# The second half of an output projection as Strassen's seven block products

## The chip, the cores and the metric

The kernel runs on one core of one Trainium2 chip. The metric is the device time of one execution in microseconds (us). Before the change it is 972.64 us, the median of 3 runs (972.55 to 972.85).

## The reference

A trunk of two decoder layers works on one sequence of 512 tokens with 1024 channels, in float32. The part that matters here is layer 1's mixer and what follows it:

```python
proj = gelu(einsum('bsd,de->bse', rms_norm(h, norm_mix[1]), w_in_odd[0]))
u, v = proj[..., :1024], proj[..., 1024:]
mix = chunked_spatial_gating(u, v, sgu_norm[0], w_spatial[0], b_spatial[0])
h = h + einsum('bse,ed->bsd', mix, w_out_odd[0])        # the output projection
hn = rms_norm(h, norm_ffn[1])
h = h + gated_conv_ffn(hn, w_ffn_gate[1], w_ffn_up[1], conv_ffn[1], b_conv_ffn[1], w_ffn_down[1])
return rms_norm(h, final_norm)
```

Layer 0 has another mixer of the same size, an output projection of the same kind, and an FFN of the same form. The hidden width of the FFN is 2816.

## The kernel before

The residual `h` is held as 8 tiles `h0` to `h7` of 128 channels by 512 tokens, float32. Every matrix product is done in float32 by three matmuls: each operand is split into a high part (rounded to the matmul's float32r) and a low part (what rounding left out), and `mm3` (lines 156 to 159) adds high by high, high by low and low by high. For weights, `parts` makes the high part by a copy on ScalarE and the low part by a subtraction on VectorE. `summed` makes the low part without VectorE: ScalarE writes the negated high part and a DMA on GpSimd's queue adds the float32 weights onto it.

Weights come through rotating buffers in the pool `wp`: 4 float32 buffers `raw`, 6 `whi` and 6 `wlo`, each of 128 partitions by 1024 elements. SyncE issues the fetches. A fetch waits until a raw buffer is free, and a split waits until a `whi` and a `wlo` buffer are free. TensorE writes to 7 PSUM banks (`mm_bank`) and one for small things.

The order of instructions on each engine is fixed when the kernel is built, by a planner that goes by the order of the program text and by its own estimate of when each operand will be ready; `inorder` and `behind` pin a few of them.

Layer 1's mixer (`mixer1`) ends like this. The group `u1` computes the last 512 columns of the input projection. Between its matmuls stand the spatial products (`spatial`) and the first transposes: `turned(j)` turns tile j of the gated product from tokens by channels to channels by tokens through TensorE (line 1106), and splits it into the high and low parts `mx` (lines 1108 and 1109). Tiles 0 to 3 are turned during `u1`, tiles 4 to 7 during the first blocks of the output projection by the hook `second_half`. The output projection is `project("oo", ...)`, in two halves of 4 output tiles. Each half takes 4 weight chunks of 256 by 512 elements and runs 4 outputs x 8 blocks x 3 = 96 matmuls of 512 tokens. The last 4 blocks are done output by output (`tail=4`), so that the outputs become ready one after another. When output tile k is ready, VectorE adds it to `h` (line 315) and `Norm.add` writes the split `hg[k]` of `h` times the gain (ScalarE line 202, VectorE line 203), squares `h` on ScalarE (lines 209 and 212), and adds the square to `ssq` on GpSimd (line 213). `hg[0]` to `hg[7]` are the FFN's moving operands.

The FFN of layer 1 (`ffn1`, `Ffn`) follows. Its first step (`direct`) multiplies with plain matmuls over the pairs 0, 4, 1, 5, 2, 6, 3, 7 and turns the residual back (`turn_residual`, line 1187) in between. From its second step on (f = 2) the FFN already works by Strassen's seven products, in the helper `multiply`: tokens are cut into two blocks of 256, and the sums over `hg` and over the weights are prepared by `block_sums` and `prepare`. One product of step f = 2 is 12 matmuls of 256 tokens (line 581). The table `BANK` says which products share a PSUM bank: 1, 6, 7 and 4 accumulate in one, 5 and 3 in another, 2 has its own.

Of the kernel before, what the change touches and what calls it, by code (L numbers as in the profile page):

```python
# [8 lines left out]
F32 = mybir.dt.float32  # L9
F32R = mybir.dt.float32r  # L10
BF16 = mybir.dt.bfloat16
AF = mybir.ActivationFunctionType
ALU = mybir.AluOpType
PSUM = bass.MemoryType.PSUM

P = 128
D = 1024
S = 512
NK = D // P
# [12 lines left out]
def tile_trunk(ctx: ExitStack, tc: tile.TileContext, x, norm_mix, norm_ffn, final_norm,  # L32
# [3 lines left out]
    nc = tc.nc  # L36
    x = x[0]
# [92 lines left out]
    def fetch(src, a, b, name):  # L130
        raw = wp.tile([P, a, b], F32, tag="raw", bufs=4, name=f"raw_{name}")
        nc.sync.dma_start(raw, src)
        return raw, a, b, name
# [52 lines left out]
    h = [cp.tile([P, S], F32, tag=f"h{k}", name=f"h{k}") for k in range(NK)]  # L186
    hg2 = [cp.tile([P, 2, S], F32R, name=f"hg{k}") for k in range(NK)]
    hg = [(t[:, 0], t[:, 1]) for t in hg2]
# [114 lines left out]
    def project(name, w, acts, ks, norm, before=None, halves=(0, 1), tail=4):  # L303

        for gi in halves:
            chunks = half_weights(name, w, ks, gi)

            def lhs(k, j):
                hi, lo, n = chunks[k]
                cs = slice(j * P, (j + 1) * P)  # L310
                return hi[:, n, cs], lo[:, n, cs]

            def done(j, ps):
                k = gi * 4 + j
                nc.vector.tensor_tensor(h[k], ps, h[k], ALU.add)  # L315
                if norm is not None:
                    norm.add(k)

            group(f"{name}{gi}", range(4), ks, lhs, lambda k, j: acts[k], tail, done,
                  before if gi == 0 else None)  # L320
# [221 lines left out]

    STEPS = [(0, None, True), (2, (0, 2, 0), False), (4, (0, 2, 1), True)]
    for f in range(6, NF, 4):
        STEPS += [(f, (f - 4, f, 0), False), (f + 2, (f - 4, f, 1), f + 4 < NF)]
    HALF = S // 2
    NP = NK // 2
# [42 lines left out]
    class Ffn:  # L592
# [109 lines left out]
        def moving(self, product, kp):  # L702

            if product in (1, 2, 3):
                k = kp if product == 1 else kp + NP
                c = slice(HALF, S) if product == 3 else slice(0, HALF)
                return hg[k][0][:, c], hg[k][1][:, c]
            if product in (6, 7):
                t = self.t23[kp][product - 6]
                return t[:, 0, :], t[:, 1, :]  # L710
            return tuple(t[:, {4: 0, 5: 1}[product], :] for t in self.t41[kp])
# [186 lines left out]
    def mixer1(norm):  # L898
        w = w_in_odd[0]
        with tc.tile_pool(name="m1", bufs=1) as mp:  # L900
# [27 lines left out]
            banks = v_group(0, {(4, 0): lambda: norm.rstd_cols(inorder)})  # L928
# [46 lines left out]
            class InProducts:  # L975
# [19 lines left out]
                def put(self, product, how, at):  # L995
                    self.stat[product] = [how(raw, 2, 512, f"{self.name}_{product}_{n}")
                                          for n, raw in enumerate(self.raw[at])]
# [18 lines left out]
                def multiply(self, banks, i, product):  # L1016
                    at = BANK[product], i
                    first = at not in banks
                    if first:
                        banks[at] = mm_bank(f"{self.name}_{at[0]}{i}")  # L1020
                    left = tokens(product, i)
                    for kp in range(NP):
                        lhs = left(kp)
                        rhs = [x[:, kp % 2, :] for x in self.stat[product][kp // 2]]
                        for l, r, end in ((0, 0, False), (0, 1, False), (1, 0, kp == NP - 1)):
                            nc.tensor.matmul(banks[at], lhs[l], rhs[r], start=first, stop=end,  # L1026
                                             skip_group_check=True)
                            first = False
                    return banks[at]
# [29 lines left out]
            v = [mp.tile([P, D], F32, tag="v", bufs=4, name=f"v{t}") for t in range(NT)]  # L1059
# [13 lines left out]
                                                   op0=ALU.mult, op1=ALU.subtract)  # L1073
                vn.append((hi, lo))

            u, gt, mix = {}, {}, {}

            def by_chunk(ap):
                return ap.rearrange("p (n c) -> p n c", c=P)
# [19 lines left out]
            def turned(j):  # L1099
                half, i = j // 4, j % 4  # L1100
                if i == 0:
                    mix["t", half] = [mp.tile([P, 4, S], F32R, tag="vn", bufs=4,
                                              name=f"mx{half}_{n}") for n in range(2)]
                ps = mm_bank(f"mT{j}")
                for t in range(NT):
                    nc.tensor.transpose(ps[:, t * P : (t + 1) * P], gt[j][:, t, :], ident)
                hi, lo = (x[:, i, :] for x in mix["t", half])
                nc.scalar.activation(hi, ps, AF.Copy)
                nc.vector.tensor_tensor(lo, ps, hi.bitcast(F32), ALU.subtract)
                mix[j] = hi, lo  # L1110

            u[0] = mp.tile([P, NT, S], F32, tag="u", bufs=2, name="u0")

# [49 lines left out]
            def second_half(k):  # L1163
                if 1 <= k < 4:
                    for j in ((4,), (5,), (6, 7))[k - 1]:
                        turned(j)

            nxt = Norm("f1", lambda k: prm1("ffn", k))
            project("oo", w_out_odd[0], mix, list(range(NK)), nxt, before=second_half)
            return nxt  # L1170


# [274 lines left out]
```

## Time and profile before

| | |
|---|---|
| median of 3 runs | 972.64 us |
| profiled execution | 972.66 us |
| its span, first to last instruction | 970.9 us |
| mean granted TensorE clock | 0.998 |
| TensorE busy | 961.0 us (99%) |
| VectorE busy | 812.9 us (84%) |
| ScalarE busy | 597.5 us (62%) |
| GpSimd busy | 152.0 us (16%) |

In the profile PE is TensorE's matmuls, PEld its weight loads, DVE VectorE, ACT ScalarE, POOL GpSimd, and SPq and POOLq the DMA issues on SyncE's and GpSimd's queues. Times are microseconds from the start of the span. A row of the timeline gives start, duration, engine, line of the kernel, and the operation with its output, inputs and shape; a bracket tells how long the engine had been idle and what released it. A row of a window gives the length of the stretch and each engine's busy time in it with its count of instructions, then the granted clock, the DMA engines' busy share and GB/s. Matmuls are pipelined, so the distance between two starts tells more than the duration of one.

### The profile page before, as it was taken

To read this page: it belongs to the slowest core of one execution; us is meant where nothing else is said; L and a number is where in the kernel's file an instruction comes from. 1 tells how busy PE (TensorE), PEld (TensorE's weight loads), DVE (VectorE), ACT (ScalarE), POOL (GpSimd) and SP (SyncE) were. 2 spreads that over 40 slices of the span, in tenths; PEclk is the share of its full clock that TensorE was granted. 3 is DMA by queue.
4 is the path that set the end of the run, shared out by engine and by line. 5 is a ranking of instruction groups with operands and counts; after the bars stand their busy time and mean duration, and the time that the engine had idled before them with its cause. 6 is when DMAs were issued, how large, how long until landed. Compare 5 with 4: busy or idle time off the path is not lost.

```text
span 970.9 us, 13658 instructions
## 1 busy us (share of the span) xinstructions
PE 961.0 (99%) x4952; PEld 818.6 (84%) x4952; DVE 812.9 (84%) x1387; ACT 597.5 (62%) x895; POOL 152.0 (16%) x173
## 2 busy tenths in 40 slices
PE   9999999999999999999999999999999999999996
PEld 7888888988888888888888888889888888888885
DVE  6887458999898998998878675589998989889897
ACT  5523347765675665765586834587665666656775
POOL 3141023110111010110311001221111011100123
PEclk9999999999999999999999999999999999999999
DMA  7442225776777677774352333167767777668775
GB/s 252 149 137 86 87 88 111 178 180 161 195 175 168 157 174 195 168 176 135 128 153 87 109 109 108 51 136 182 185 142 196 195 174 174 159 162 200 195 154 139
DMA packets 92335, 148.33 MB, mean 153 GB/s; under 512 B 5124, under 2 KB 56300, under 8 KB 92268
## 3 DMA queue, kind: packets, MB, share of 16 engines
q1 hardware_dynamic: 76236, 98.69, 32.1%
q0 software_dynamic: 14256, 46.93, 26.8%
q10 hardware_dynamic: 1776, 1.84, 0.6%
q8 instruction: 39, 0.64, 0.3%
q14 instruction: 28, 0.23, 0.1%
HBM read 98.42 MB, written 2.10 MB: 104 GB/s over the span
## 4 chain that ended last, share of the span: by engine, by line
PE 94%; DVE 3%; DMA 1%; issue 1%; ACT 0%; POOLq 0%; DVEq 0%; POOL 0%
PE dn L158 3%; PE dn L159 3%; PE dn L157 3%; PE d L158 3%; PE d L157 3%; PE d L159 3%; PE vu_a L1026 2%; PE gu L157 2%; PE gu L159 2%; PE oo L159 2%; PE oo L157 2%; PE gu L158 2%; PE oe L159 1%; PE oe L158 1%; PE oo L158 1%; PE oe L157 1%
## 5 line engine op out<-in xcount | busy, mean ns | idle before, releaser
L144 POOL DMA_DIRECT2D wlo_g<-raw_g x20 | 17.2, 862 | 318.8 <-ACT wlo_g L142 118.3
L617 DVE SCALAR_TENSOR_TENSOR c<-rows,prm,c 128x512 f32<-128x512 f32 x88 | 65.3, 744 | 1.6 <-ACT c L615 1.4
L158 PE MATMUL dn<-wlo_dn,a_hi 128*128 128x512 f32 x144 | 56.2, 390 | 0.0
L158 PE MATMUL d<-a_lo,whi_d 128*128 128x512 f32 x144 | 56.2, 390 | 0.0
L159 PE MATMUL dn<-whi_dn,a_lo 128*128 128x512 f32 x144 | 56.2, 390 | 0.0
L159 PE MATMUL d<-a_hi,wlo_d 128*128 128x512 f32 x144 | 56.1, 390 | 0.0
L157 PE MATMUL d<-a_hi,whi_d 128*128 128x512 f32 x144 | 56.1, 390 | 0.0
L157 PE MATMUL dn<-whi_dn,a_hi 128*128 128x512 f32 x144 | 56.1, 390 | 0.0
L731 ACT ACTIVATE whi_a<-raw_g 128x512 fp32r<-128x512 f32 x20 | 12.6, 632 | 61.3 <-PE g_10e L571 9.0
L213 POOL TENSOR_TENSOR ssq_f<-ssq_f,sq_f 128x512 f32<-128x512 f32 x14 | 19.8, 1411 | 142.4 <-issue 102.0
L142 ACT ACTIVATE wlo_g<-raw_g 128x1024 fp32r<-128x1024 f32 x20 | 21.2, 1062 | 27.5 <-PE g_2e L581 8.8
L202 ACT ACTIVATE hg<-h,prm 128x512 fp32r<-128x512 f32 x24 | 17.3, 721 | 33.1 <-DVE h L315 33.1
L615 ACT ACTIVATE c<-rows,prm 128x512 f32<-128x512 f32 x44 | 31.4, 715 | 9.8 <-DVE rows L828 9.6
L625 ACT ACTIVATE s<-c,prm 128x512 f32<-128x512 f32 x44 | 31.4, 716 | 6.2 <-DVE c L617 6.1
L1201 DVE SCALAR_TENSOR_TENSOR y<-dn,small,y 128x512 f32<-128x512 f32 x40 | 28.0, 749 | 8.1 <-PE dn L159 8.1
L203 DVE SCALAR_TENSOR_TENSOR hg<-h,prm,hg 128x512 fp32r<-128x512 f32 x24 | 22.6, 944 | 11.9 <-ACT hg L202 11.9
L159 PEld LDWEIGHTS dn<-whi_dn,a_lo 128*128 128x128 f32 x144 | 27.0, 188 | 5.7
L159 PEld LDWEIGHTS d<-a_hi,wlo_d 128*128 128x128 f32 x144 | 27.0, 188 | 5.7
L153 DVE TENSOR_TENSOR wlo_dn<-raw_dn,whi_dn 128x1024 fp32r<-128x1024 f32 x18 | 22.0, 1224 | 11.7 <-ACT whi_dn L152 10.6
L157 PEld LDWEIGHTS d<-a_hi,whi_d 128*128 128x128 f32 x144 | 27.1, 188 | 5.4
L157 PEld LDWEIGHTS dn<-whi_dn,a_hi 128*128 128x128 f32 x144 | 27.1, 188 | 5.4
L158 PEld LDWEIGHTS dn<-wlo_dn,a_hi 128*128 128x128 f32 x144 | 27.0, 188 | 5.4
(1060 smaller groups left out, 3261.6 us busy)
## 6 DMA issues: line engine op xcount, KB each, us to landing
raw_g<-in_w_ffn_gate_dram SPq DMA_DIRECT2D x40, 512.0 KB, 3.8
raw_u<-in_w_ffn_up_dram SPq DMA_DIRECT2D x40, 512.0 KB, 4.3
raw_dn<-in_w_ffn_down_dram SPq DMA_DIRECT2D x22, 512.0 KB, 6.0
wlo_g<-raw_g POOLq DMA_DIRECT2D x20, 512.0 KB, 4.6
wlo_u<-raw_u POOLq DMA_DIRECT2D x20, 512.0 KB, 6.4
raw_d<-in_w_ffn_down_dram SPq DMA_DIRECT2D x18, 512.0 KB, 4.1
wlo_s12g<-s12g POOLq DMA_DIRECT2D x18, 512.0 KB, 6.3
wlo_s34g<-s34g POOLq DMA_DIRECT2D x18, 512.0 KB, 5.7
```

Of the source, the lines that this page charges most:

```text
L142: first = nc.scalar.activation(lo, raw, AF.Copy, scale=-1.0)
L153: behind(nc.vector.tensor_tensor(lo, raw, hi.bitcast(F32), ALU.subtract), after[0])
L157: nc.tensor.matmul(ps, lhs[0], rhs[0], start=start, stop=False)
L158: nc.tensor.matmul(ps, lhs[0], rhs[1], start=False, stop=False)
L159: nc.tensor.matmul(ps, lhs[1], rhs[0], start=False, stop=stop)
L203: nc.vector.scalar_tensor_tensor(hg[k][1], h[k], g, hg[k][0].bitcast(F32), op0=ALU.mult, op1=ALU.subtract)
L213: nc.gpsimd.tensor_tensor(self.ssq, self.ssq, sq, ALU.add)
L615: nc.scalar.activation(c, t[:, 0:S], AF.Copy, scale=prm("cf", ft))
L617: self.last_conv = nc.vector.scalar_tensor_tensor(c, t[:, i : S + i], prm("cf", i * NF + ft), c, op0=ALU.mult, op1=ALU.add)
L625: self.last_silu = nc.scalar.activation(s, c, AF.Silu, bias=self.prm("bf", ft))
L1026: nc.tensor.matmul(banks[at], lhs[l], rhs[r], start=first, stop=end, skip_group_check=True)
L1201: return nc.vector.scalar_tensor_tensor(dst, ps, ffn.cols[:, t : t + 1], dst, op0=ALU.mult, op1=ALU.add)
```

## The change

The first half of layer 1's output projection stays. The second half (output tiles 4 to 7) is cut into blocks: output channels in two of 256, input channels in two of 512, tokens in two of 256. It is computed by seven block products in the order 1, 2, 6, 5, 7, 3, 4, each for two output tiles of 128 channels, and each of these is 12 matmuls of 256 tokens.

- The weights are fetched as 4 blocks of 512 by 256. `parts` splits the weights of products 1, 2, 4 and 6, `summed` those of 5, 7 and 3. Four sums of blocks are made in place on VectorE.
- `turned` also writes a float32 copy of each turned tile (`mr`, in the buffers of the tag `v`) on ScalarE.
- `sums_of`, called from the hook at blocks 4 and 5 of the first half, makes the sums of token blocks in place on VectorE. Two of the four sums are split into `hg[4]` to `hg[7]`, which are free at that time (products 6 and 5); the other two into new tiles `t43` in the buffers of the tag `u` (products 4 and 7), with the low part by ScalarE and a DMA on GpSimd's queue.
- After each product VectorE adds the bank to half a tile of `h`, 14 additions of 256 tokens. After products 3 and 4 `norm.add` follows for the tile.

```diff
+    def block_sums_of(y0, y1):
+        t3, t1, t2, t4 = y1[:, :, HALF:], y0[:, :, HALF:], y0[:, :, :HALF], y1[:, :, :HALF]
+        nc.vector.tensor_tensor(t3, t3, t1, ALU.subtract)
+        nc.vector.tensor_tensor(t1, t1, t2, ALU.subtract)
+        nc.vector.tensor_tensor(t2, t2, t3, ALU.add)
+        nc.vector.tensor_tensor(t4, t4, t2, ALU.subtract)
+
+    def project_blocks(name, w, acts, sums, norm):
+        raw = {}
+        for i, j in ((0, 0), (1, 0), (1, 1), (0, 1)):
+            raw[i, j] = fetch(w[i * 512 : (i + 1) * 512, 512 + j * HALF : 512 + (j + 1) * HALF]
+                              .rearrange("(k p) c -> p k c", p=P), 4, HALF, f"{name}_{i}{j}")
+        stat = {}
+        def put(product, how, at):
+            r, a, b, n = raw[at]
+            stat[product] = how(r, a, b, f"{n}_{product}")
+        def to(at, x, y, op):
+            nc.vector.tensor_tensor(raw[at][0], raw[x][0], raw[y][0], op)
+
+        a11, a12, a21, a22 = (0, 0), (1, 0), (0, 1), (1, 1)
+        put(1, parts, a11)
+        put(2, parts, a12)
+        put(4, parts, a22)
+        to(a22, a21, a22, ALU.add)
+        to(a21, a11, a21, ALU.subtract)
+        to(a11, a22, a11, ALU.subtract)
+        put(6, parts, a11)
+        to(a12, a12, a11, ALU.subtract)
+        put(5, summed, a22)
+        put(7, summed, a21)
+        put(3, summed, a12)
+
+        def moving(product, kp):
+            if product in (1, 2, 3):
+                c = slice(HALF, S) if product == 3 else slice(0, HALF)
+                return tuple(x[:, c] for x in acts[kp + (0 if product == 1 else NP)])
+            return sums[product](kp)
+
+        banks = ({}, {})
+        for product in (1, 2, 6, 5, 7, 3, 4):
+            for i in range(2):
+                hi, lo = stat[product]
+                c = slice(i * P, (i + 1) * P)
+                ps = multiply(banks[i], f"{name}_{i}", product,
+                              lambda kp: (hi[:, kp, c], lo[:, kp, c]),
+                              lambda kp: moving(product, kp))
+                k = 4 + i + 2 * (product in (5, 7, 4))
+                d = h[k][:, HALF:] if product in (6, 5, 7, 3) else h[k][:, :HALF]
+                nc.vector.tensor_tensor(d, ps, d, ALU.add)
+                if product in (3, 4):
+                    norm.add(k)
...
             def turned(j):
...
                 mix[j] = hi, lo
+                if i % 2 == 0:
+                    whole[half].append(mp.tile([P, 2, S], F32, tag="v", bufs=4, name=f"mr{j}"))
+                nc.scalar.copy(whole[half][-1][:, i % 2, :], ps)
...
             def second_half(k):
                 if 1 <= k < 4:
                     for j in ((4,), (5,), (6, 7))[k - 1]:
                         turned(j)
+                elif k in (4, 5):
+                    sums_of(k - 4)
+
+            t43 = []
+            def sums_of(q):
+                y0, y1 = whole[0][q], whole[1][q]
+                block_sums_of(y0, y1)
+                for n in range(2):
+                    hi, lo = hg[4 + 2 * q + n]
+                    nc.scalar.activation(hi, y0[:, n, :], AF.Copy)
+                    nc.vector.tensor_tensor(lo, y0[:, n, :], hi.bitcast(F32), ALU.subtract)
+                t = mp.tile([P, 2, 2, S], F32R, tag="u", bufs=2, name=f"t43_{q}")
+                nc.scalar.activation(t[:, 1], y1, AF.Copy, scale=-1.0)
+                nc.gpsimd.dma_start(t[:, 1], y1, accum_op=ALU.add)
+                nc.scalar.activation(t[:, 0], y1, AF.Copy)
+                t43.append(t)
 
             nxt = Norm("f1", lambda k: prm1("ffn", k))
-            project("oo", w_out_odd[0], mix, list(range(NK)), nxt, before=second_half)
+            project("oo", w_out_odd[0], mix, list(range(NK)), nxt, before=second_half, halves=(0,))
+
+            def late(kp, c):
+                return tuple(t43[kp // 2][:, i, kp % 2, c] for i in range(2))
+
+            project_blocks("oo1", w_out_odd[0], mix,
+                           {6: lambda kp: tuple(x[:, :HALF] for x in hg[4 + kp]),
+                            5: lambda kp: tuple(x[:, HALF:] for x in hg[4 + kp]),
+                            4: lambda kp: late(kp, slice(0, HALF)),
+                            7: lambda kp: late(kp, slice(HALF, S))}, nxt)
```

More of the change, by code (lines that the diff above doesn't have):

```diff
@@ L1074, in v_normed @@
                 vn.append((hi, lo))
-            u, gt, mix = {}, {}, {}
+            u, gt, mix, whole = {}, {}, {}, ([], [])
             def by_chunk(ap):
```

## The prediction, made before the changed kernel ran

> **What bounds the kernel now.** I read the page first, then the chain of waits around the changed stage, then the timeline of each engine there. The page says which engine sets the time.
>
> ```profile
> span 970.9 us, 13658 instructions
> PE 961.0 (99%) x4952; PEld 818.6 (84%) x4952; DVE 812.9 (84%) x1387; ACT 597.5 (62%) x895; POOL 152.0 (16%) x173
> PE 94%; DVE 3%; DMA 1%; issue 1%; ACT 0%; POOLq 0%; DVEq 0%; POOL 0%
> ```
>
> TensorE is on the chain for 94% of the span, so the sum is a count of TensorE time in the changed stage plus whatever TensorE is made to wait. Where the stage begins and ends is in TensorE's timeline; the last two rows are from layer 1's first block-product step (f = 2), which already runs products of the new shape.
>
> ```profile
> 599.98 0.39 PE L157 MATMUL oo<-mx,whi_oo 128*128 128x512 f32 x1
> 621.75 1.04 PE L1187 MATMUL hT<-ident,h 128*128 128x128 f32 x8
> 649.96 0.40 PE L581 MATMUL u_2a<-hg,whi_a 128*128 128x256 f32 x2
> 651.40 0.40 PE L581 MATMUL g_2b<-hg,whi_g 128*128 128x256 f32 x2
> ```
>
> The second half of the output projection runs from 599.98 to 621.75, which is 21.77 us for 96 matmuls of 512 tokens (4 outputs, 8 blocks, 3 each), 0.2268 us apiece. One product of 12 matmuls of 256 tokens takes 651.40 - 649.96 = 1.44 us, 0.12 us apiece. Half the width costs 53% of the time.
>
> The other engines in the stretch before the projection and in its two halves, and the engines' durations that I use below:
>
> ```profile
> core 0: us, PE busy (x) PEld busy (x) DVE busy (x) ACT busy (x) POOL busy (x), PEclk, DMA share, GB/s
> 558.00:576.40 18.40, 18.40 (x91) 15.25 (x90) 12.48 (x20) 6.59 (x9) 0.00 (x0) 1.00 0.34 115
> ...
> 576.40:600.00 23.60, 23.60 (x114) 19.61 (x113) 14.18 (x18) 10.23 (x15) 1.72 (x2) 1.00 0.29 90
> 600.00:621.80 21.80, 21.80 (x98) 18.00 (x97) 11.49 (x13) 8.93 (x14) 5.60 (x5) 1.00 0.31 97
> ```
>
> TensorE has no gap and full clock; VectorE is busy for 14.18 of 23.60 us and then 11.49 of 21.80, ScalarE for less. There is room in both, but the change uses it at particular times.
>
> **The change part by part.** *TensorE.* Removed are the 96 wide matmuls, 21.77 us. Added are 7 products x 2 output blocks x 12 narrow ones, 14 x 1.44 = 20.16 us. The difference is -1.61 us. It is the whole possible gain: 7/8 of the arithmetic, less most of what narrower matmuls lose.
>
> The Trainium skill speaks on this in "TensorE: Matmul & The Clock Gate", section "Back-to-back issue gap": a warm isolated matmul takes its width over 2.4 GHz plus 2.5 ns, so 216 ns and 109 ns. By that the stage would go from 20.7 to 18.3 us, a gain of 2.4 us. No row here shows it: the trace has 226.8 and 120 ns.
>
> *Weights.* Four `parts` remain four (products 1, 2, 4, 6). The three `summed` are new: two ScalarE copies and a GpSimd accumulating DMA each. The four block sums `to` are new on VectorE. Rows for these and the sums over tokens:
>
> ```profile
> 582.32 1.06 ACT L152 ACTIVATE whi_oo<-raw_oo 128x1024 fp32r<-128x1024 f32 x1 [2.00 <-PE oo L158]
> 583.41 1.22 DVE L153 TENSOR_TENSOR wlo_oo<-raw_oo,whi_oo 128x1024 fp32r<-128x1024 f32 x1 [1.50 <-ACT whi_oo L152]
> 584.55 0.68 DVE L1109 TENSOR_TENSOR mx<-mT,mx 128x512 fp32r<-128x512 f32 x1
> 586.13 1.09 ACT L1108 ACTIVATE mx<-mT 128x512 fp32r<-128x512 f32 x2 [2.27 <-PE mT L1106]
> 586.76 1.29 DVE L1109 TENSOR_TENSOR mx<-mT,mx 128x512 fp32r<-128x512 f32 x2 [1.53 <-ACT mx L1108]
> 589.08 1.06 ACT L152 ACTIVATE whi_oo<-raw_oo 128x1024 fp32r<-128x1024 f32 x1 [1.86 <-PE oo L158]
> 592.02 0.69 DVE L315 TENSOR_TENSOR h<-oo,h 128x512 f32<-128x512 f32 x1 [0.63 <-PE oo L159]
> 592.75 0.72 ACT L202 ACTIVATE hg<-h,prm 128x512 fp32r<-128x512 f32 x1 [2.61 <-DVE h L315]
> 593.38 0.62 ACT L209 ACTIVATE ssq_f<-h 128x512 f32<-128x512 f32 x1
> 593.50 0.75 DVE L203 SCALAR_TENSOR_TENSOR hg<-h,prm,hg 128x512 fp32r<-128x512 f32 x1 [0.79 <-ACT hg L202]
> 600.18 0.69 DVE L315 TENSOR_TENSOR h<-oo,h 128x512 f32<-128x512 f32 x1 [0.49 <-PE oo L159]
> 639.49 0.68 DVE L752 TENSOR_TENSOR s12g<-raw_g,raw_g 128x512 f32<-128x512 f32 x1
> L804 DVE TENSOR_TENSOR rows<-g_4a,rows 128x256 f32<-128x256 f32 x5 | 2.1, 421 | 0.3 <-ACT rows L816 0.2
> ```
>
> So a 512-wide sum is 0.68 us, a 256-wide add from PSUM 0.42, a 1024-wide low part 1.22. No float32 sum of 1024 elements stands here; the nearest are the 1.22 and two of 512, 1.36; I take 1.22.
>
> *VectorE, whole change.* Added: 4 `to` x 1.22 = 4.9, 8 token sums x 0.68 = 5.4, 4 low parts into `hg` x 0.68 = 2.7, and 14 adds x 0.42 for 4 x 0.69, 3.1: 16.1 us into 19.7 us of idle time. *ScalarE*: 6 copies of 1024 in `summed` and 4 for `t43`, 10 x 1.06 = 10.6, 8 float32 copies `mr` and 4 `hg` copies x about 0.6 = 7.2: 17.8 us into 26.2. Both fit, so what counts is the first place where the added work is due.
>
> *The tight place: product 6.* Its weights come out of a chain on VectorE (three `to`, then the low part), its tokens out of `sums_of`, which needs the turned tiles 4 to 7. The last transposes before that, and the last tiles' halves, stand at 586.13 to 588.05. Product 6 starts after products 1 and 2 at 599.98 + 4 x 1.44 = 605.74 and needs its low weights two matmuls later, at 605.98. From the end of the low part of tile 5 (584.55 + 0.68 = 585.23) VectorE has 20.75 us. Its work up to there: two low parts of turned tiles 1.29; 8 sums 5.44; 4 `hg` low parts 2.72; add and gain for h0 to h3, 4 x (0.69 + 0.75) = 5.76; three `to` 3.66; the low part of product 6, 1.22; product 1's two adds 0.84. Together 20.93 us, 0.18 over. If h3's 1.44 and the adds' 0.84 come behind it, it is 2.1 early: that is the bound below, no wait. ScalarE's share of the same stretch (tiles 1.09, hg 2.4, `t43` 4.24, norm 4 x 1.34, product 6's copy 1.06, late `mr` copies 1.2: 15.4 us) fits.
>
> On top of that VectorE is slowed by GpSimd:
>
> ```profile
> 625.20 1.39 POOL L213 TENSOR_TENSOR ssq_f<-ssq_f,sq_f 128x512 f32<-128x512 f32 x1 [2.57 <-ACT sq_f L212]
> 625.35 1.52 DVE L686 TENSOR_TENSOR t<-t 128x256 f32<-128x256 f32 x1
> 626.79 0.41 DVE L687 TENSOR_TENSOR t<-t 128x256 f32<-128x256 f32 x1
> ```
>
> The same 256-wide operation takes 1.52 beside the GpSimd add and 0.41 behind it, so a meeting costs up to 1.1 us. Three such adds (h1 to h3) fall into the stretch. I take one full meeting, 1.1, between none and 3.3. Product 6 is then 0.18 + 1.10 = 1.28 us late. TensorE runs its queue in order, so products 6, 5, 7, 3, 4 and layer 1's FFN all wait behind it; VectorE and ScalarE catch up meanwhile.
>
> The Trainium skill's "SBUF — State Buffer", section "Who interferes with whom", has the pair of ports as a lock: a VectorE instruction with two SBUF inputs waits for the whole of a GpSimd instruction that reads SBUF. The 1.52 agrees. With all three adds met in full by this rule, the sum would be 974.5.
>
> *Products 5, 7, 3* need low weights from accumulating DMAs:
>
> ```profile
> 632.32 1.07 ACT L142 ACTIVATE wlo_g<-raw_g 128x1024 fp32r<-128x1024 f32 x1
> wlo_g<-raw_g POOLq DMA_DIRECT2D x20, 512.0 KB, 4.6
> wlo_s12g<-s12g POOLq DMA_DIRECT2D x18, 512.0 KB, 6.3
> ```
>
> A weight slot comes free at 599.98 at the latest (six of each half, and the copies at 582.32 and 589.08 waited just so for the projection's matmuls). Behind 2.40 us of other ScalarE work (0.72 + 0.62 + 1.06) the copy ends at 603.45, and 6.3 us later, 609.75, the low part is there; product 5 wants it at 599.98 + 6 x 1.44 + 0.24 = 608.86. That is 0.89 late with 6.3, in time with 4.6, and under the 1.28 in any case, which it doesn't add to. Products 7 and 3 follow 2.88 us apart each and the copies 2.13, so they are no tighter.
>
> *Around it.* Edits at nothing: the `mr` copies of tiles 0 to 3 run ahead of 576.4, where ScalarE is busy for 6.59 of 18.40 us; the transposes are the same; PSUM needs 6 banks of 7. The raw buffers are held until the sums are done, so SyncE's fetches of the FFN's first weights move from
>
> ```profile
> 577.55 0.89 SPq L640 DMA_DIRECT2D raw_g<-in_w_ffn_gate_dram  x2
> 591.42 0.88 SPq L640 DMA_DIRECT2D raw_u<-in_w_ffn_up_dram  x2
> raw_g<-in_w_ffn_gate_dram SPq DMA_DIRECT2D x40, 512.0 KB, 3.8
> 622.54 0.47 PE L157 MATMUL gu<-hg,whi_g 128*128 128x512 f32 x1
> 626.42 0.87 PE hT L1187 x8
> 633.67 0.79 PE ssc_f L230 x8
> ```
>
> to about 607.5 for the first (when `to` has read block 11). 607.5 + 3.8 + 1.06 + 1.22 = 613.6, 9 us before the 622.54 at which it is used; without that cover each us late would be a us. Five more DMA issues stand on GpSimd's queue between its `ssq` adds; the sum of squares is due at 633.67, 12 us after the stage. The turned h4 to h7 are due at 626.42, 4.7 us after it, and want one add of 0.42.
>
> *Sum.* -1.61 + 1.28 = -0.33. The profiled execution took 972.66 us (span 970.9 and 1.76 around it), the median of the runs is 972.64; 972.64 - 0.33 = 972.3 us. About 0.2%, 1.95 us, is what a measurement of this kernel can tell from no change, so this is "the same".
>
> **The rivals.** *Full cover:* VectorE takes product 6's chain ahead of h3's norm and the adds; no wait, 972.64 - 1.61 = 971.0. For it: 2.1 us of the 20.93 need not be ahead. Against: nothing in the program puts the chain first.
>
> *VectorE late (slower).* The order on VectorE is settled ahead of the run, sums and norms first. If the chain stands behind all of it, it begins when h3's add ends, 600.18 + 0.69 = 600.87, and takes 3.66, then 1.06 on ScalarE in which nothing else fills VectorE, 1.22, the adds 0.84 and three GpSimd meetings 3.3: 610.95, so 4.97 late, net +3.36, 976.0. It turns to "slower" from a wait of 1.61 + 1.95 = 3.56 us. For it: the budget is full to 1%. Against: VectorE has short waits before 600 into which `to` fits.
>
> *DMAs one after the other.* If the three accumulating DMAs don't overlap, they land at 609.75, 616.05 and 622.35; products 7 and 3 are due at 611.74 and 614.62, so 4.3 and, shifted, 3.4 late: 7.7 in all, net +6.1, 978.8. Against: landings of 4.6 to 6.3 are medians of a queue that has two in flight.
>
> *Narrow matmuls cheaper than 0.12 us.* The saving becomes 2.4 us, 970.2. Against: the two rows of that shape above, at 1.44 a dozen. By the Trainium skill's gap above it would be so; the trace doesn't bear it.
>
> **How the numbers follow.** Forecast case (a wait between 0.3 and 3.5 us) 0.45; full cover 0.18; VectorE late 0.22; DMAs in series 0.07; narrow matmuls cheaper 0.03; something not named, slower, 0.05. Same is 0.45 + 0.18 = 0.63, slower 0.22 + 0.07 + 0.05 = 0.34, faster 0.03. The forecast's own range is 971.3 to 974.5. The range for 8 in 10 takes in full cover and VectorE late, 970.9 to 976.6; left out are series, the cheap matmuls and the unnamed case, 0.15.
>
> **What would show it.** In the profile after: 14 products at 1.44 us; a gap of about 1.3 us on TensorE ahead of the first product 6 matmul with VectorE's `wlo` of product 6 as its releaser, and none ahead of 5, 7, 3, 4; VectorE above 90% busy from 585 to 606; the stage about 21.4 us instead of 21.77; FFN without new gaps. It is wrong if the gap stands ahead of product 5 or 7 with a DMA as releaser, if it is beyond 3.56 us, or if time is lost before 600 or after the stage.

## The result and the profile after

The changed kernel takes 979.1 us (median of 6 runs; 978.9 to 979.65), the kernel before 972.67 us beside it on the same chip. The ratio is 1.0066, with a 95% interval of 1.0053 to 1.0079: slower by 6.4 us, outside the forecast's 970.9 to 976.6. The page after, in the same three rows as before:

```profile
span 977.2 us, 13881 instructions
PE 963.0 (99%) x5024; PEld 823.0 (84%) x5024; DVE 828.1 (85%) x1413; ACT 613.1 (63%) x917; POOL 157.0 (16%) x178
PE 95%; DVE 2%; DMA 1%; issue 1%; ACT 1%; POOL 1%; POOLq 0%; DVEq 0%; SPq 0%
```

The page hides the loss: TensorE has 95% of the chain and 99% of the span, where it had 94% and 99% before. The view of waits shows it, asked for TensorE from 598 to 660 us (total, times, longest). Before, this view has no row there. In a bank's name the digit is the output tile of the pair and the letter the bank of the table `BANK`. After:

```profile
PE oo_1e L637 <- DVE h L597: 2.5, 1, 2.5
PE oo_0e L637 <- DMA wlo_oo<-raw_oo: 1.1, 2, 0.8
PE oo_0a L637 <- DMA wlo_oo<-raw_oo: 0.7, 1, 0.7
```

The timeline of TensorE gives their places (a bracket is the idle time before the row and what ended it; the moving operand tells the products apart: `hg` is 6 and 5, `t` is 7 and 4, and `mx` with `oo_0e` or `oo_1e` is 3):

```profile
600.23 0.40 PE L637 MATMUL oo_0a<-mx,whi_oo 128*128 128x256 f32 x2
605.98 0.44 PE L637 MATMUL oo_0a<-hg,whi_oo 128*128 128x256 f32 x2
609.87 0.38 PE L637 MATMUL oo_0e<-hg,wlo_oo 128*128 128x256 f32 x1 [0.35 <-DMA wlo_oo<-raw_oo]
613.75 0.39 PE L637 MATMUL oo_0a<-t,wlo_oo 128*128 128x256 f32 x1 [0.75 <-DMA wlo_oo<-raw_oo]
617.66 0.38 PE L637 MATMUL oo_0e<-mx,wlo_oo 128*128 128x256 f32 x1 [0.77 <-DMA wlo_oo<-raw_oo]
621.62 0.79 PE L637 MATMUL oo_1e<-mx,whi_oo 128*128 128x256 f32 x2 [2.51 <-DVE h L597]
624.34 0.48 PE L637 MATMUL oo_0a<-t,whi_oo 128*128 128x256 f32 x2
627.29 0.93 PE L1272 MATMUL hT<-ident,h 128*128 128x128 f32 x7
```

The stage runs from 600.23 to 627.29, 27.06 us in place of 21.77. Without waits it would be the 20.16 of the forecast, so 6.90 us are lost inside. By the distances between the starts of the half products (each 1.44 us without loss): product 6 loses 0.25 in all, the first halves of 5, 7 and 3 lose 0.61, 1.01 and 1.02 to DMAs, the wait ahead of product 3's second half is 2.67, and that half itself takes 624.34 - 621.62 = 2.72 instead of 1.44, another 1.28. The windows say why that half is slow (the third figure from the end is the granted clock, as a share of full speed, and the one behind it the DMA engines' busy share):

```profile
619.00:621.60 2.60, 0.10 (x1) 0.00 (x0) 1.60 (x3) 2.03 (x2) 0.00 (x0) 0.90 1.06 339
621.60:624.30 2.70, 2.68 (x12) 2.68 (x13) 2.70 (x4) 1.06 (x1) 0.00 (x0) 0.50 0.66 196
```

From 621.0 on, 2 us into the wait, the clock was granted at 0.50. The long wait itself is read from the other engines' timelines (the last row is SyncE's queue):

```profile
618.91 1.06 ACT L152 ACTIVATE whi_u<-raw_u 128x1024 fp32r<-128x1024 f32 x1 [6.43 <-DMA raw_u<-in_w_ffn_up_dram]
620.00 1.22 DVE L153 TENSOR_TENSOR wlo_u<-raw_u,whi_u 128x1024 fp32r<-128x1024 f32 x1 [5.92 <-ACT whi_u L152]
621.15 0.42 DVE L597 TENSOR_TENSOR h<-oo_1e,h 128x256 f32<-128x256 f32 x1
609.88 1.67 SPq L696 DMA_DIRECT2D raw_u<-in_w_ffn_up_dram  x2
```

VectorE stood idle for 5.92 us ahead of the low part of an FFN weight, whose fetch was issued at 609.88 and whose data ScalarE got at 618.91. Behind it in VectorE's order stood the addition of product 5, oo_1e, and product 3's second half needs that bank. So TensorE waited for a weight that it would use only in the FFN. The FFN's start (up to the first product of f = 2) took 27.04 us (26.78 before), and step f = 2 took 20.16 (20.15).

### The profile page after: what moved, and what is told of

Read it like the earlier page. It is cut to its first block, busy times and chain, and to the rows that moved or that the text cites. A ratio compares the mean times of both kernels' runs of the same rounds, so it can differ in the third digit from the quotient of the medians.

```text
span 977.2 us, 13881 instructions
## 1 busy us (share of the span) xinstructions
PE 963.0 (99%) x5024; PEld 823.0 (84%) x5024; DVE 828.1 (85%) x1413; ACT 613.1 (63%) x917; POOL 157.0 (16%) x178
## 4 chain that ended last, share of the span: by engine, by line
PE 95%; DVE 2%; DMA 1%; issue 1%; ACT 1%; POOL 1%; POOLq 0%; DVEq 0%; SPq 0%
PE dn L158 3%; PE dn L159 3%; PE d L158 3%; PE d L157 3%; PE dn L157 3%; PE d L159 3%; PE vu_a L1082 2%; PE gu L157 2%; PE gu L159 1%; PE gu L158 1%; PE oe L159 1%; PE oe L158 1%; PE oe L157 1%; PE u_2a L637 1%; PE u_4a L637 1%; PE g_2a L637 1%
## 5 line engine op out<-in xcount | busy, mean ns | idle before, releaser
L266 ACT ACTIVATE a_hi<-s 128x512 fp32r<-128x512 f32 x40 | 24.8, 626 | 10.7 <-PE d L159 7.7
```

The costliest lines, as they stand in the source:

```text
L266: nc.scalar.activation(hi, src, AF.Copy, scale=scale)
```

## The experiments

Three theories are told apart in what follows. **Q**: an in-order engine holds an instruction that TensorE needs behind one that isn't needed yet. **D**: the three accumulating DMAs are late. **R** and **T**: the lateness has another source (late weights, or VectorE without slack), so that it comes back wherever the order is mended. The table gives TensorE's three stretches in each profiled run, as distances of starts: stage, FFN's start, step f = 2; then the median time and the ratio to the kernel before, which ran beside each of them (its median was 972.62 to 972.79).

| kernel | stage | FFN's start | f = 2 | us | ratio |
|---|---|---|---|---|---|
| before | 21.77 | 26.78 | 20.15 | 972.67 | 1 |
| changed | 27.06 | 27.04 | 20.16 | 979.10 | 1.0066 [1.0053, 1.0079] |
| e1 | 23.03 | 32.81 | 20.16 | 981.35 | 1.0091 [1.0078, 1.0104] |
| e2 | 22.64 | 26.80 | 20.16 | 973.66 | 1.0011 [1.0002, 1.0020] |
| e5 | 20.38 | 30.96 | 20.15 | 975.63 | 1.0038 [1.0026, 1.0050] |
| e6 | 20.94 | 33.59 | 20.15 | 979.11 | 1.0068 [1.0055, 1.0081] |
| e7 | 20.37 | 27.22 | 22.31 | 974.37 | 1.0018 [1.0009, 1.0027] |
| e8 | 23.02 | 29.28 | 22.29 | 979.08 | 1.0066 [1.0053, 1.0080] |
| e9 | 21.76 | 26.78 | 20.16 | 972.86 | 1.0002 [0.9993, 1.0011] |
| e10 | 21.14 | 29.28 | 22.02 | 976.65 | 1.0044 [1.0032, 1.0057] |
| e12 | 20.38 | 27.92 | 21.05 | 973.18 | 1.0006 [0.9997, 1.0015] |
| e5b | 20.37 | 28.73 | 20.16 | 973.87 | 1.0015 [1.0007, 1.0024] |
| e13 | 23.61 | 26.81 | 20.15 | 974.88 | 1.0021 [1.0012, 1.0030] |
| e15 | 22.36 | 27.06 | 20.75 | 973.85 | 1.0012 [1.0004, 1.0021] |
| e16 | 21.48 | 27.07 | 20.76 | 973.24 | 1.0005 [0.9996, 1.0014] |

The diffs show the lines that decide; lines that only record instructions, such as `last_add`, are left out.

**e1: the FFN's low parts behind the additions.** On VectorE the low parts of u0, g1 and u1 (the FFN's later weights) come behind product 7's second addition.

```diff
-                ch[key, half] = parts(raw, 4, 2 * P, name)
+                ch[key, half] = parts(raw, 4, 2 * P, name, after=(last_add[7]
+                    if self.layer and (key, half) != ("g", 0) else None, None))
```

> One edit to the changed kernel: on VectorE the low parts of three of the FFN's first four weight tiles (u of the first half, g and u of the second) are put behind product 7's second addition. Theory Q (the queue): TensorE's 2.51 us wait ahead of the second half of product 3, and the 1.28 us that its twelve matmuls take longer at half the granted clock behind that wait, come from VectorE's fixed order, where the low part of u, whose weights land at 618.9, stands ahead of product 5's addition. Then both go: 979.1 - 3.9 = 975.2 us (974.6 to 976.0), granted clock 1.0 through the stage, the DMA waits of 0.6, 1.0 and 1.0 us ahead of products 5, 7 and 3 stay. Rival D (late transfers as such): the weights are late whatever the order, the wait moves to the FFN's first u matmuls, 977.5 or more.

The wait ahead of product 3 and the slow clock are gone, 4.0 us off the stage, as Q says. But the kernel is slower, not faster, and the total is where D put it (977.5 or more), though the new waits name no weight: the wait moved behind the stage (view of waits, then VectorE's timeline):

```profile
PE hT L1272 <- DVE h L597: 2.6, 1, 2.6
PE gu L157 <- ACT y L1274: 1.5, 1, 1.5
624.46 2.00 DVE L153 TENSOR_TENSOR wlo_u<-raw_u,whi_u 128x1024 fp32r<-128x1024 f32 x1
628.06 0.41 DVE L597 TENSOR_TENSOR h<-oo_0a,h 128x256 f32<-128x256 f32 x1
```

Now product 4's addition runs at 628.06, 5 us after product 4 ended, behind the same low parts and two norm splits. In the stretch from 632 to 635 us the granted clock was 0.60.

**e2: no accumulating DMAs.** Products 5, 7 and 3 are split by `parts`.

```diff
-        put(5, summed, a22)
-        put(7, summed, a21)
-        put(3, summed, a12)
+        put(5, parts, a22)
+        put(7, parts, a21)
+        put(3, parts, a12)
```

> One edit to the changed kernel: the low parts of products 5, 7 and 3 are made on VectorE (parts) and not by GpSimd's DMA (summed). Rival D (the accumulating DMAs are the whole cause: they are late themselves, hold the raw buffers and so the FFN's fetches): all waits go, 971.3 to 972.6 us. Theory Q (VectorE's fixed order decides): the three low parts, 3.66 us, stand ahead of product 1's additions, and product 6 goes to the same bank, so TensorE waits about 4.8 us ahead of product 6, with a clock drop of about 1.3 us behind it, and no longer ahead of 5, 7 and 3: 976 to 978 us.

973.66 us lies between the two forecasts: nearly the whole loss went, more than Q allows, and less than all, which D wanted. With `parts`, the raw buffers are free as soon as VectorE has read them; SyncE issued the FFN's four fetches at 605.31, 607.50, 609.33 and 610.43, against 605.55 to 615.79 in the changed kernel. So the `summed` splits did three things. They were late themselves. By holding the raw buffers they made the FFN's fetches start later. And those fetches took longer: the first one for `u` landed after 8.2 us in the changed kernel and after 2.7 here (view of DMAs). From 604 to 620 us the accumulating DMAs took 56.8% of the DMA engines' time in the changed kernel and the fetches 37.9%, together all but 5% of it; here the fetches took 67.5% and nothing else of note ran. The three low parts on VectorE have their own price, and the order that was built put product 5 ahead of product 6:

```profile
PE oo_0e L637 <- DVE wlo_oo L153: 1.4, 1, 1.4
PE oo_0a L637 <- DVE h L597: 0.6, 1, 0.6
```

**e5: the splits late and the FFN's low parts behind.** As e2, each of the three splits behind the additions of products 1, 2 and 6, and e1's edit.

```diff
+            if product in late:        # {1: (5, a22), 2: (7, a21), 6: (3, a12)}
+                put(late[product][0], parts, late[product][1], after=(last_add[product], None))
```

> The two edits together, with the order settled by hand: the low parts of 5, 7 and 3 on VectorE, each put behind the additions of products 1, 2 and 6, and the FFN's low parts behind product 7's additions. Theory Q: nothing that a product needs stands behind something late, so no wait is left, the stage is 14 x 1.44 = 20.2 us: 972.67 - 1.6 + 0.3 = 971.4 us (971.0 to 972.2). Rival V (VectorE has not the time for 3.66 us more up to product 3): waits of 0.5 to 1 us ahead of several products, 973 to 975 us. Rival D expects no difference from the parts alone.

The stage is at 20.38 us with no wait: the saving of TensorE that was forecast is there, 1.39 of 1.61 us. It is lost in the FFN's start, by the same moved wait as in e1, and the total, 975.63, is above all that was expected:

```profile
PE gu L157 <- ACT y L1274: 1.5, 1, 1.5
PE hT L1272 <- DVE h L595: 0.5, 1, 0.5
627.00:629.60 2.60, 2.60 (x11) 2.26 (x12) 2.60 (x4) 1.77 (x4) 1.48 (x2) 0.57 0.00 0
```

**e6: `summed` kept, its DMAs first on GpSimd.** e1's edit, and the additions of squares of the first half behind the three DMA issues.

```diff
         put(3, summed, a12)
+        for ins in norm.adds:
+            behind(ins, summed_dma[0])
```

> The first experiment's edit, and on GpSimd's queue the additions of squares for h1 to h7 are put behind the three accumulating DMAs of products 5, 7 and 3. If the DMAs are late because they are issued late, behind additions of squares that take 1.8 us each beside a busy VectorE, the first is issued at 602.7 and not 604.3, the waits ahead of products 5, 7 and 3 fall from 2.6 us to below 1: 973.2 to 974.2 us. If they are late because the transfers themselves are slow (5.5 to 9.4 us to landing), nothing changes against the first experiment: 975.2 us.

GpSimd's timeline in the changed kernel, and then in e6, with the one wait for a DMA that TensorE's view has there:

```profile
600.77 3.62 POOL L213 TENSOR_TENSOR ssq_f<-ssq_f,sq_f 128x512 f32<-128x512 f32 x2 [1.07 <-ACT sq_f L212]
604.34 0.86 POOL L144 DMA_DIRECT2D wlo_oo<-raw_oo  x1
```

```profile
602.96 0.86 POOL L145 DMA_DIRECT2D wlo_oo<-raw_oo  x1 [3.29 <-ACT wlo_oo L143]
607.92 2.98 POOL L214 TENSOR_TENSOR ssq_f<-ssq_f,sq_f 128x512 f32<-128x512 f32 x2
PE oo_0a L640 <- DMA wlo_oo<-raw_oo: 0.3, 1, 0.3
```

The first issue is 1.38 us earlier, and what the DMAs cost falls, by distances, from 2.64 us to 0.79 (0.57 ahead of product 7, 0.22 ahead of product 3). So the DMAs were late in the main because they were issued behind two additions of squares, which took 1.8 us each beside VectorE. The total, 979.11, lies above both forecasts, because the FFN's start is worse than in e1.

**e7 and e8: all additions first.** The low parts of g1 and u1 come behind product 4's last addition; e7 is e5 so changed, e8 is e1 (with `summed`).

```diff
-after=(last_add[7] if ...
+after=(last_add[4 if half else 7] if ...
```

> The late-parts kernel (products 5, 7 and 3 split by parts, each behind the additions of products 1, 2 and 6), and now also the FFN's low parts of g1 and u1 behind product 4's last addition; u0's stays behind product 7's. Theory Q (the loss is where the low parts of late FFN weights stand in VectorE's order, ahead of the product additions): the stage stays at 20.4 us, the FFN's start up to the first product of step f = 2 falls from 30.96 to about 26.8 us, and the total is 972.7 - 1.4 = 971.3 us (971.0 to 972.2). Rival R (the FFN's start is late by the weights themselves, which are fetched late whatever VectorE's order): the wait returns ahead of the FFN's matmuls with u or g1, total 973.5 to 975.6. Rival C (seven products in place of 96 wide matmuls don't save TensorE time once the waits are gone): 972.7 or more with no wait in either stretch.

> The changed kernel with summed kept for products 5, 7 and 3, the FFN's low part of u0 behind product 7's last addition and those of g1 and u1 behind product 4's. Theory Q: the stage as with the first edit of this kind, 23.0 us (three DMA waits of 1.9 together stay), the FFN's start 26.8 to 27.4 us instead of 32.8, total 981.35 - 5.7 = 975.6 us (974.8 to 976.5). Rival R (late weights): the FFN's start stays over 30 us and the total over 978.

In e7 the stage (20.37) is as Q says and the FFN's start (27.22) 0.4 above, but 3.1 us more than expected are on the total. 2.16 of them are in step f = 2, which takes 22.31 us instead of 20.15. Its waits, and ScalarE's timeline there:

```profile
PE g_2a L637 <- ACT rows L872: 1.6, 2, 1.4
656.27 1.28 ACT L681 ACT_TABLE_LOAD   x1 [0.66 <-DVE c L673]
657.56 1.34 ACT L681 ACTIVATE s<-c,prm 128x512 f32<-128x512 f32 x2
659.59 0.36 ACT L872 COPY rows<-g_2a 128x256 f32<-128x256 f32 x1
```

It is the same thing on ScalarE: the copy that frees the bank of product 6 stands behind a table load that waited for VectorE's `c`. e8 lies 3.5 us above Q's 975.6, in which the DMA waits were counted: beside the loss in f = 2 it has a wait of 1.7 for ScalarE's copies of the turned residual (`y`), which stand behind four norms in a row. Both times fall where R put them, but not for its reason, late weights: neither kernel has a weight as releaser in the FFN's start.

**e10: e8 with e6's DMAs first.**

> The changed kernel, summed kept, with its three accumulating DMAs issued ahead of the first half's additions of squares on GpSimd, and the FFN's low parts of u0, g1, u1 behind the additions of products 7, 4 and 4 on VectorE. Theory Q with the GpSimd queue as the second cause: stage 20.9 us as when the DMAs were put first, FFN's start 26.8 to 27.4, total 972.7 - 0.8 + 0.4 = 972.3 us (971.5 to 973.2). Rival R (late weights): total 976 or more. Rival S (the delayed additions of squares are due earlier than thought): a wait ahead of the reciprocal root of the sum of squares, 974 to 976.

The stage is 21.14, as Q says, and the FFN's start has e8's wait of 1.7, f = 2 e8's wait of 1.4. None of the theories had these two. The time lies where R put it, but again no weight is a releaser.

**e9: the token sums alone.** The kernel before, with the copies `mr`, `sums_of` and `t43` added and the second half left as it was; nothing uses the sums.

> The kernel before (plain second half of 96 wide matmuls, its weights by parts, FFN fetches where they were) with only the preparation of the tokens added: the float32 copies of the turned tiles, the sums over token blocks, their split into hg[4] to hg[7] and t43 with the two accumulating DMAs; nothing uses the sums, so the output is the same. If the added VectorE, ScalarE and GpSimd work is hidden: 972.7 us (972.4 to 973.2). If it costs the early 0.25 us and the later 0.3 us that the changed kernel loses outside the stage: 973.2 to 973.5. If the meetings of VectorE with GpSimd are what delays the sums in the changed kernel: over 974.

972.86 us, 1.0002 [0.9993, 1.0011]: hidden. TensorE has no wait, and the windows (compare the prediction's) show the added work in idle time, VectorE 20.48 us instead of 14.18:

```profile
576.40:600.00 23.60, 23.60 (x113) 19.63 (x112) 20.48 (x29) 17.43 (x26) 1.98 (x3) 1.00 0.46 121
```

**e12: e7 with that copy first.** The two activations of the FFN's first step come behind the copy of product 6 on ScalarE.

```diff
+                    [behind(x, ins) for x in self.silus[:2]
+                     if self.layer and f == 2 and (key, product) == ("g", 6)]
```

> The all-additions-first kernel (parts for products 5, 7, 3, FFN low parts behind the additions of products 7, 4, 4), and on ScalarE in step f = 2 the two sigmoid-linear activations of the FFN's first step (with the table load of 1.28 us) behind the copy of product 6's bank. Theory Q (what is left of the loss is the same kind of thing, a copy that frees a PSUM bank standing behind late work on an in-order engine, now on ScalarE): the 1.43 us wait ahead of the g product 7 of step f = 2 goes, the step takes 20.2 to 20.4 us instead of 22.31, the total is 974.37 - 1.43 - 0.2 to 0.5 = 972.4 to 972.9, and TensorE's waits between 598 us and the end are under 0.3 us in sum: no difference from before, with about 0.4 us of the 1.61 left. Rival T (VectorE has no idle time left from 637 to 660 us, so the wait only changes its name): a wait of 1 to 2 us on VectorE's additions or the first step's activations, 973.8 to 974.8.

973.18 us, no difference from before that can be measured (the interval holds 1). The wait of 1.43 is gone as Q says; others of 0.6, 0.2 and 0.2 stand in the FFN's start and in f = 2, 1.0 us in all where Q had under 0.3. The total, 973.2, lies 0.3 above Q's range and 0.6 below T's.

**e5b: the late splits without anything on the FFN's low parts.**

> The changed kernel with products 5, 7 and 3 split by parts, each behind the additions of products 1, 2 and 6, and nothing done to the FFN's low parts, which the order puts among the additions of products 5, 7 and 3 on VectorE. Theory Q (it matters which instruction stands ahead of an addition, and whether its weights are there by then): without the summed DMAs the raw buffers come free earlier, so the FFN's low parts stand in the way for less; product 3's second half waits at most 1 us and the FFN's start loses 1 to 3 us, total 972.5 to 975. Rival D (only the DMA splits cost anything): 971.0 to 972.0. Rival R (the late FFN weights cost as much as in the changed kernel whatever the splits): 977 or more.

The stage is 20.37, without a wait, although the FFN's low parts stand among the additions, the one of u0 one addition later than in the changed kernel: the weights are there in time now. The first fetch for `u` was issued at 609.01, only 0.87 us earlier than in the changed kernel, but ScalarE had its data at 612.68 and not at 618.91, because it landed after 2.9 us and not 8.2. So the order alone costs nothing in the stage; it costs where what stands ahead waits for a late transfer, and most of that lateness was the length of the transfer, with the accumulating DMAs beside it. The total is in Q's range (972.5 to 975); D (971 to 972) and R (977 or more) are both out. In the FFN's start one wait is left, 1.41 us (VectorE's timeline):

```profile
622.10 3.02 DVE L203 SCALAR_TENSOR_TENSOR hg<-h,prm,hg 128x512 fp32r<-128x512 f32 x2
625.05 0.41 DVE L595 TENSOR_TENSOR h<-oo_1a,h 128x256 f32<-128x256 f32 x1
```

Two norm splits, 0.75 us each when alone, took 3.02 beside GpSimd's additions of squares. All four residual tiles become complete in the last two products, where the kernel before has one complete every 2.7 us.

**e13 and e15: product 3 ahead of product 7**, so that two tiles are complete 2.9 us earlier; e13 is e5b so changed (the late splits follow the same order), e15 has e7's and e12's order edges as well.

```diff
-        for product in (1, 2, 6, 5, 7, 3, 4):
+        for product in (1, 2, 6, 5, 3, 7, 4):
```

> The late-parts kernel with product 3 ahead of product 7 (order 1, 2, 6, 5, 3, 7, 4), so that h4 and h5 are complete 2.9 us earlier than h6 and h7; nothing else. Theory B (with the stage's waits gone, what eats the saving is that all four residual tiles become complete in the last two products, so four norms and the residual's turning pile up on VectorE, ScalarE and GpSimd at the FFN's start, where the kernel before has one tile complete every 2.7 us): the FFN's start falls from 28.73 to 26.8 to 27.3 us, the wait of 1.41 us there goes, total 973.87 - 1.5 to 1.9 = 972.0 to 972.4 us. Rival L (the FFN's low parts in VectorE's order are the cost, whoever is complete first): the wait of 1 to 1.5 us stays, 973.2 to 974.2. Rival E (product 3 right behind product 5 waits for product 5's addition, which shares its bank): a wait of 0.5 to 1 us ahead of product 3, total 973 or more.

> All that has helped, together: products 5, 3, 7 split by parts and late, product 3 ahead of product 7, the FFN's low parts of u0 behind product 7's additions and of g1 and u1 behind product 4's, and the two activations of the FFN's first step behind the copy of product 6 in step f = 2. Theory B: stage 20.4 us, FFN's start 26.8 to 27.3, step f = 2 at 20.2 to 20.5, total 972.7 - 1.4 + 0.2 to 0.7 = 971.5 to 972.0, ratio 0.999. Rival T (VectorE without slack in the FFN's start): 972.6 to 973.4, no better than without the change of order.

The FFN's start falls to 26.81 and 27.06, as theory B (the norms piled up) says. The totals, 974.88 and 973.85, are above what B gave. In e13 the figure is within rival E's (973 or more), but there is no wait ahead of product 3, which was E's reason; e15 is above T's range too. The stage got a wait of 1.5 ahead of product 6 in both, and e13 another, of 1.5, ahead of the second half of product 4. e15's view names ScalarE for the first; VectorE's timeline has another candidate:

```profile
PE oo_0a L637 <- ACT whi_oo L152: 1.5, 1, 1.5
605.51 1.77 DVE L203 SCALAR_TENSOR_TENSOR hg<-h,prm,hg 128x512 fp32r<-128x512 f32 x1
607.20 0.41 DVE L595 TENSOR_TENSOR h<-oo_0a,h 128x256 f32<-128x256 f32 x1
```

**e16: e15 with product 1's additions ahead of h3's norm split.**

```diff
+                if product == 1:  behind(norm.last_lo, last_add[1])
```

> The kernel with all that has helped, and the split of h3's norm on VectorE behind product 1's two additions, because the 1.49 us that TensorE waited there ahead of product 6 ended when the addition of product 1 (at 607.20) had run behind that split (605.51, 1.77 us beside GpSimd), although the view names ScalarE's copy. Theory A (the addition that frees the bank was the wait): the wait goes, the stage takes 20.4 to 20.7 us instead of 22.36, the total is 973.85 - 1.5 = 972.3 us (971.7 to 972.7), at or just under the kernel before. Rival W (it was ScalarE's copy of the weights, as the view names it): the wait stays, 973.4 to 974.2. Rival T (VectorE has no slack between 600 and 660 us, so a wait that goes returns later): the wait goes and the total stays over 973.

The wait is gone, and ScalarE's two copies, which end at 607.45, didn't move against the stage's start; TensorE began product 6 at 605.86. So it waited for the addition (theory A), and the releaser that the view named was wrong. But the total, 973.24 us, fell by 0.6 and not by 1.5, which the two intervals hardly tell apart from no change: waits of 0.5 and 0.4 for VectorE's additions are now ahead of products 3 and 4 (rival T's kind). The windows of the stage, of the FFN's start and of f = 2 show why (VectorE is the third busy time):

```profile
600.00:621.00 21.00, 20.18 (x166) 19.76 (x165) 17.51 (x25) 12.86 (x17) 7.50 (x5) 1.00 0.54 151
621.00:648.00 27.00, 27.00 (x145) 22.61 (x144) 20.95 (x42) 21.36 (x41) 8.63 (x9) 1.00 0.59 125
648.00:670.00 22.00, 21.83 (x175) 21.30 (x174) 21.28 (x34) 17.80 (x27) 2.59 (x3) 1.00 0.58 152
```

VectorE is busy for 17.51 of 21 us where it was 11.49 of 21.80 before. Behind that it goes into the FFN, where it is busy for 20.95 of 27 and then 21.28 of 22. In the kernel before it was busy for 20.16 and 20.94 there, so these stretches were nearly as full already, and lateness that is carried into them is not made up. No version tried beats the kernel before; e12 and e16 are level with it.

## Why the prediction was wrong

**What held.** TensorE's saving: 14 half products at 1.44 us each where nothing waited, and e5's stage of 20.38 us against 20.16. That the token sums are hidden (e9: +0.2 us, not to be told from nothing). That VectorE would be above 90% busy from 585 to 606 us: from 585.2 on it has no gap there, and yet TensorE has no wait for it. That product 6 would start on time at best: its first matmul is at 605.98, 5.75 us after the stage's start, where 5.76 was due.

**The forecast wait ahead of product 6, 1.28 us, didn't come;** 0.25 us were lost inside product 6. Of the two readings of the budget, "2.1 early" was the right one, since the chain ran ahead of h3's norm and of product 1's additions, and of the norms of h1 and h2 too. VectorE's timeline after has the low part of product 6 done at 600.85, 5 us ahead of its use:

```profile
599.64 1.21 DVE L153 TENSOR_TENSOR wlo_oo<-raw_oo,whi_oo 128x1024 fp32r<-128x1024 f32 x1
600.77 2.46 DVE L203 SCALAR_TENSOR_TENSOR hg<-h,prm,hg 128x512 fp32r<-128x512 f32 x2
```

The rival "full cover" had this right and nothing else.

**Step "Products 5, 7, 3" failed on the cover, on the issue and on the landings.** It put the first DMA right behind its ScalarE copy, ending at 603.45, and its landing at 609.75. The copy ended at 602.70, the issue came at 604.34, behind the additions of squares (shown by e6), although the prediction's own text has GpSimd's queue, and the landing was at 609.84: for product 5 the time was right by luck, two errors against each other. The step let the 1.28 us of product 6 cover what was late; the cover never existed. It then called products 7 and 3 "no tighter", with 6.3 us for each landing; the three landings took 5.5, 7.1 and 9.4. The term, costed at nothing, was 2.64 us.

**Step "Around it" is the one that lost the forecast.** It followed one fetch, the first of the FFN's weights, found 9 us of cover for its use by TensorE, and stopped. Eight fetches move, the third and fourth (u0) to 609.88, and those two don't land after the 3.8 us that the step took from its own row but after 8.2, with the DMA engines full (a busy share of 1.05 from 608 to 616 us). And the first to suffer isn't TensorE's use of the weight in the FFN but VectorE's order, in which the low part of u0 stands ahead of product 5's addition. The term, costed at nothing, was 2.67 us of waiting and, with the clock, 1.28 more. That is shown from two sides: e1 takes the low parts out of the way and the wait goes from the stage, e5b makes the weights earlier and it goes too. The late weights weigh more than the order: without accumulating DMAs and with no order edge on the FFN's weights (e2, e5b), 5.4 and 5.2 of the 6.4 us come back, while e1's order edge, with the DMAs kept, lost more than it won. That the slow landings come from the DMAs running beside them is read from the traces that have them (8.2, 8.2 and 7.4 us in the changed kernel, e1 and e6) and those that don't (2.7 and 2.9 in e2 and e5b); no run has changed that alone.

**The clock** had no term. Together: 20.16 + 0.25 + 2.64 + 2.67 + 1.28 = 27.00 of the 27.06 us measured. 0.25 us more stand ahead of the stage, where the profiled runs of the changed kernels differ by 1.1 among themselves (it starts at 600.54 in e5b and at 599.46 in e10), and 0.26 in the FFN's start; some 0.45 of the profiled run's difference lie behind the last matmul, after 968 us, and their cause is open.

The prediction's list of what would show it wrong had it: a gap ahead of products 5 and 7 with a DMA as releaser. The case was there as the rival of DMAs one after another (978.8, chance 0.07), with the wrong mechanism: they overlapped, each issued before the one ahead of it had landed, and the cost was 2.64 us and not 7.7.

**Where the saving goes when the order is mended** was in none of the cases: four norms at once at the FFN's start, and a VectorE with 16 us of added work up to the stage's end and no slack behind it. Each order edge that removed a wait gave part of it back later, or more than all of it (e1, e5, e7, e16).

## What to carry to other kernels

When a change moves a fetch, follow everything that reads it, first of all the split that stands in an in-order engine's queue, and ask what stands behind that split; the use of the weight by TensorE may come last. Of an accumulating DMA count the issue, behind what its engine is doing then, the time for which its source buffer stays taken, and what else needs the DMA engines while it runs. A saving of 1.6 us on an engine that is 99% busy is real only if the others keep their slack: adding 16 us of work to VectorE made the order of every addition matter.

## What the hardware did that was not expected

The clock halved behind a gap of 2.5 us: 12 matmuls of 256 tokens took 2.72 us instead of 1.44, with 0.50 granted. The length of one gap doesn't decide it. A gap of 2.6 us in e1 (ending at 628.52) left the clock at 1.00 for over 2 us, and it fell only with a second one of 1.5 right after it; gaps of 0.5 and 1.5 close together gave 0.57 (e5); single gaps of 1.4 (e5b) and 1.7 us (e8) had no such effect. Where it fell, it stayed at 0.50 for about 3.4 us (621.0 to 624.5 in the changed kernel, 630.9 to 634.3 in e1, 627.3 to 630.7 in e5) or for twice that (627.2 to 634.0 in e6). The Trainium skill, "TensorE: Matmul & The Clock Gate", section "What's actually happening", has the half clock after an idle window of about 3.4 us that runs on by itself; the lengths of the slow spells agree, and the gaps ahead of them were all shorter than 3.4. How much of a window has to be idle isn't shown by these runs.

An accumulating DMA holds the DMA engines for longer than a fetch. From 604 to 620 us in the changed kernel the three took 56.8% of the engines' time for 1.57 MB, and the fetches beside them 37.9% for 2.06 MB: about twice the time for each byte.

Two additions of squares on GpSimd took 3.62 us beside a busy VectorE, and single ones 1.3 to 1.4 (e15); VectorE's norm splits took 1.5 each beside GpSimd (e5b), where they take 0.75 alone. Each engine was slower beside the other, so norms that are piled up cost more than norms one by one.
